# Attention's output projection: head sums made beside the scores, and a third pair of k with seven block products

## The chip, the cores and the metric

The kernel runs on one core of a Trainium2 chip. The time is the device time of one execution, in microseconds (us); three runs of the kernel before are given by their median. One further execution was profiled, and all rows quoted below come from it. Its engines: PE multiplies matrices, DVE and ACT work element by element, POOL and SP mostly issue transfers. Each engine takes its instructions in the order in which they stand in its own list, and waits at the first whose inputs are not there.

## The reference, cut to what matters

Two layers over 256 positions of width 2048. Layer 0 mixes tokens with a gated spatial MLP; layer 1, the one that matters here, with attention over 16 heads in blocks of 128 queries, whose outputs go through one square projection. After each mixer comes a layer norm, then a gated MLP with a short convolution, then another norm.

```python
def chunk_causal_attention(q_nope, q_rope, k_nope, k_rope, v):
    for qb in range(S // Q_BLOCK):
        ...
        s = s.astype(jnp.float32) * SM_SCALE
        ...
        p = jax.nn.softmax(s, axis=-1).astype(v.dtype)
        outs.append(jnp.einsum('bhqk,bkhd->bqhd', p, v[:, :k_end]))
...
    o = chunk_causal_attention(q_nope, q_rope, k_nope, k_rope, v)
    return o.reshape(B, S, MLA_HEADS * V_DIM) @ w_out
...
x = layer_norm(ALPHA * x + m, ln_mix_g[i], ln_mix_b[i])
f = conv_ffn(x, ffn_w_up[i], ffn_conv_w[i], ffn_conv_b[i], ffn_w_down[i])
```

Everything is float32, and the result must agree with that.

## The kernel before, in words

**Products.** A float32 product is made of rounded parts: each operand is split into a high part (a cast on ACT, L127) and a low part (a subtraction on DVE, L130), and three PE matmuls of 128x512 add hi*hi, lo*hi and hi*lo. Splitting the weights as they stream in is therefore the standing work of ACT and DVE. A chunk of weights is one 1 MB load into one of three "raw" buffers, and its parts (`wh`, `wl`) take two of 14 "big" slots, which also hold the attention's keys (`knT`), its outputs (`oT`), the residual and the normed input (`xhl`) of the next product.

**Eight or seven.** A chunk covers two blocks of k and 1024 columns, so 2x2 row blocks by 2x2 column blocks: eight block products, 24 matmuls. Marked `seven`, it is multiplied with seven block products (a Strassen-like form), 21 matmuls: then the weights' sums (`ts`, `th`, `tl`, L137 and L127/L130) must be made and split too, and so must sums of the other operand (`combine`: four DVE subtractions and additions by `turn`, a cast, a subtraction). `MO_SEVEN` names the pairs of k for which the second half of the attention's output projection does so.

**The stage around the change.** A loop over t runs the heads as a pipeline. Step t makes the scores of head t (`attend_a`: `sc` on PE; then ACT copies a piece, DVE masks, adds and takes maxima, ACT takes exponentials, DVE scales `p`), transposes p of head t-1 (`attend_b`: `pt` on PE, `pts` on ACT), multiplies head t-2 by the values (`attend_c`: `o` on PE, split into `oT`), and between these multiplies head t-4 by its weights for the first 1024 columns of the projection (`mo`, L232). The weights' chunks are numbered 298 to 305 for this half and 306 to 313 for the second 1024 columns (`mo_q`, `mo_p`, `mo_e`). With the last heads through, `sum_heads` makes the sums of the pairs 1 and 2 (heads 2, 3 and 4, 5), in the last two steps of the loop. Chunks 307 and 308 use them.

**The boundary behind it.** `boundary` finishes the four accumulators of the second half one after another (block 0 then block 1 of rows), adds each to the residual (`piece`: DVE L666 and a `BN_STATS`), aggregates (`start`: `BN_AGGR`, a root on ACT, a reciprocal), normalizes (`scale`: DVE L681), transposes (`put`: `lnt` on PE), applies gain and bias (`lny`, ACT L726) and splits (`xhl`, L729 and L730). Then `upf`, the first group of the next product, can start. Chunks 314 and up are its weights.

**What sets the order.** The instructions of an engine are not written out by hand: a scheduler orders them at build time by its own estimate of when inputs are ready, with earlier program text first. On the chip that order is fixed.

Of the kernel before, what the change touches and what calls it, by code (L numbers as in the profile page):

```python
# [8 lines left out]
F32 = mybir.dt.float32  # L9
# [6 lines left out]
P = 128  # L16
S = 256
# [7 lines left out]
H = 16  # L25
# [26 lines left out]
U_PAIRS = [[0, 1, 5, 7, 2, 6, 3, 4]] + [[0, 1, 2, 5, 3, 7, 4, 6]] * 5  # L52
U_SEVEN = [(2, 3)] + [(2, 3, 4)] * 4 + [(2, 3)]

MO_SEVEN = (1, 2)

T1, T2 = 6, 5
SLOTS = {"big": 14, "raw": 3, "side": 6}
# [153 lines left out]
def trunk(ctx: ExitStack, tc: tile.TileContext, x, xT, gm_in, gm_wout, ffn_up, ffn_dn,  # L212
# [5 lines left out]
    tp = ctx.enter_context(tc.tile_pool(name="tp", bufs=3))  # L218
# [6 lines left out]
    def slot(shape, name, dt=F32, tag="big"):  # L225
        return big.tile(shape, dt, tag=tag, name=name, bufs=SLOTS[tag])
# [47 lines left out]
    chunks += [(ml_b[i], 2048, "") for i in range(ml_b.shape[0])]  # L274
    chunks += [(ml_out[i], 2048, "seven" if i - 8 in MO_SEVEN else "") for i in range(ml_out.shape[0])]
    chunks += [(ffn_up[1, i], 2048, "") for i in range(n_up)]
# [13 lines left out]
    def turn(t, k1, k2):  # L290

        at = lambda k, b: k[:, b] if len(k.shape) == 3 else k[:, b * P : (b + 1) * P]
        tc.keep_in_program_order(nc.vector.tensor_tensor(t[:, 0], at(k1, 0), at(k1, 1), ALU.subtract))
        nc.vector.tensor_tensor(t[:, 1], at(k1, 1), at(k2, 1), ALU.subtract)
        nc.vector.tensor_tensor(t[:, 2], t[:, 1], at(k1, 0), ALU.subtract)
        nc.vector.tensor_tensor(t[:, 3], at(k2, 0), t[:, 2], ALU.add)

    def combine(name, o, k1, k2):


        t = tp.tile([P, 4, P], F32, tag="t2", name=f"xs{name}", bufs=T2)
        turn(t, k1, k2)
        o = o.rearrange("p (h s c) -> p h s c", h=2, s=4)
        nc.scalar.copy(o[:, 0], t)
        nc.vector.tensor_tensor(o[:, 1], t, o[:, 0].bitcast(F32), ALU.subtract)
        return [(o[:, 0, i], o[:, 1, i]) for i in (1, 2, 0, 3)]

    for j in range(4):
        t = slot([P, 4, S], f"xraw{j}", tag="side")
# [47 lines left out]
    def x_parts(xs, k, b):  # L357
        t = xs[k // 4]
        return (t[:, k % 4, b * P : (b + 1) * P], t[:, k % 4, S + b * P : S + (b + 1) * P])

    def prod_b(acc, parts, hi, lo, pieces, first, last):

        xh, xl = parts
        for f, (o, w) in enumerate(pieces):
            mm(acc[f][:, :w], xh, hi[:, o : o + w], first, False)
            mm(acc[f][:, :w], xl, hi[:, o : o + w], False, False)
            mm(acc[f][:, :w], xh, lo[:, o : o + w], False, last)
# [385 lines left out]
    for gi in range(6):  # L753
# [3 lines left out]
        for c, p in enumerate(V_PAIRS[gi]):  # L757
            a = [[x_parts(xhl, 2 * p + j, b) for j in range(2)] for b in range(2)]
            got = feed.next()
            if p in V_SEVEN[gi]:  # L760
                acc.seven(a, xc[p], *got)
                if p == V_SEVEN[gi][-1]:
                    rest = acc.rest()
            elif gi == 0 and c < 2:
                acc.first(a, *got, c == 0)
            else:
                acc.eight(a, *got)
            if gi == 0 and p in V_SEVEN[1]:
                x4 = xraw[p // 2]
                room = xc_room[len(xc) // 2][:, len(xc) % 2, :]  # L770
                xc[p] = combine(p, room, x4[:, 2 * (p % 2)], x4[:, 2 * (p % 2) + 1])
            if c == 2 and gi > 0:
                stats(gi - 1)
            if c == 4 and gi == 0:
                nc.sync.dma_start(cst, consts)
                nc.sync.dma_start(rope_sb, ropes)
                nc.sync.dma_start(lnrow, ln_rows.rearrange("r (k p) -> (r k) p", p=P))
                nc.sync.dma_start(brow[0:NG, :], b_s.rearrange("o (g i) -> (o g) i", g=NG))
            if c == 7 and gi == 5:
                wTg = []  # L780
                for i in range(4):
                    t = tp.tile([P, 2, P], F32, tag="t1", name=f"wT{i}", bufs=T1)
                    nc.gpsimd.dma_start(t, w_sT[:, 2 * i : 2 * i + 2, :])
                    nc.gpsimd.memset(t[64:P, :, 0:64], 0.0)
                    wTg += [t[:, 0, :], t[:, 1, :]]
        vt = slot([P, 2, 1024], f"v{gi}", tag="side")
        for i, (n, t) in enumerate(zip(DIRECT, rest)):
            o = vt[:, i // 2, (i % 2) * 512 : (i % 2) * 512 + 512]
# [80 lines left out]
    for g in range(6):  # L869
# [26 lines left out]
        for i, t in enumerate(rest):  # L896
            o = v[g][:, i // 2, i % 2 * 512 : i % 2 * 512 + 512]
# [146 lines left out]
    for b in range(2):  # L1044
# [3 lines left out]
        t = tp.tile([P, 4, ROPE], F32, tag="t1", name=f"kr2_{b}", bufs=T1)  # L1048
# [117 lines left out]
    def attend_b(h):  # L1166

        p = probs[h]
        pt = bank(f"pt{h}")
        for j in range(3):  # L1170
            nc.tensor.transpose(pt[:, j * P : (j + 1) * P], p[:, j * P : (j + 1) * P], ident)  # L1171
        pts = tp.tile([P, 3 * P], F32, tag="t2", name=f"pts{h}", bufs=T2)
        nc.scalar.copy(pts, pt[:, : 3 * P])
        probs[h] = pts

    def attend_c(h):
        if h % 4 == 0:
            oT.append(slot([P, 4, 512], f"oT{h // 4}", F32R))
        pts = probs.pop(h)
        o = bank(f"o{h}")  # L1180
        c = slice(h * P, (h + 1) * P)
        mm(o[:, 0:S], vv[0][:, c], pts[:, 0:S], True, False)
        mm(o[:, P:S], vv[1][:, c], pts[:, S : 3 * P], False, True)
        hi = oT[h // 4][:, h % 4, 0:S]
        nc.scalar.copy(hi, o[:, 0:S])
        nc.vector.tensor_tensor(oT[h // 4][:, h % 4, S : 2 * S], o[:, 0:S], hi.bitcast(F32), ALU.subtract)

    for hf in range(2):
# [13 lines left out]
        for b in range(2):  # L1202
            for f in range(2):
                c = slice(hf * 1024 + f * 512, hf * 1024 + (f + 1) * 512)
# [7 lines left out]
    mo_sums, mo_room = {}, []  # L1212

    def sum_heads(c):

        if len(mo_sums) % 2 == 0:
            mo_room.append(slot([P, 2, 8 * P], f"mos{c}", F32R))
        x = oT[c // 2][:, 2 * (c % 2) : 2 * (c % 2) + 2]
        raw = tp.tile([P, 2, S], F32, tag="t2", name=f"mor{c}", bufs=T2)
        nc.vector.tensor_tensor(raw, x[:, :, 0:S].bitcast(F32), x[:, :, S : 2 * S].bitcast(F32), ALU.add)  # L1220
        mo_sums[c] = combine(f"mo{c}", mo_room[-1][:, len(mo_sums) % 2, :], raw[:, 0], raw[:, 1])

    for t in range(3, H + LAG):
        k = t - LAG
        if k >= 0:
            if k % 2 == 0:
                hi, lo = feed.next()
            w = slice((k % 2) * 1024, (k % 2) * 1024 + 1024)
        if 3 < t < H:
            attend_a(t)  # L1230
        if k >= 0:
            prod_b(acc[0], x_parts(oT, k, 0), hi[:, w], lo[:, w], halfp, k == 0, k == KD - 1)
        if t < H + 2:
            attend_c(t - 2)
        if k >= 0:
            prod_b(acc[1][:1], x_parts(oT, k, 1), hi[:, w], lo[:, w], halfp[:1], k == 0, k == KD - 1)
        if t - 1 < H:
            attend_b(t - 1)
        if 0 <= t - H - 1 < len(MO_SEVEN):
            sum_heads(MO_SEVEN[t - H - 1])  # L1240
        if k >= 0:
            prod_b(acc[1][1:], x_parts(oT, k, 1), hi[:, w], lo[:, w], halfp[1:], k == 0, k == KD - 1)
    ln.begin()
# [4 lines left out]
    mo = Banks("mo1", DIRECT + OWN)  # L1248
    acc = [[mo.acc[DIRECT[2 * b + f]] for f in range(2)] for b in range(2)]
    late = []  # L1250
    for c in range(8):
# [7 lines left out]
        a = [[x_parts(oT, 2 * c + j, b) for j in range(2)] for b in range(2)]  # L1259
        if c in MO_SEVEN:  # L1260
            mo.seven(a, mo_sums[c], *got)
        else:
            mo.eight(a, *got)
        if c == MO_SEVEN[-1]:
            for j, t in enumerate(mo.rest()):
# [107 lines left out]
```

## Time and profile before

| what | us |
|---|---|
| median of 3 runs | 2464.81 (2464.58 to 2466.5) |
| the profiled execution, its own time | 2465.45 |
| its span in the trace | 2463.7 |
| PE busy | 2456.6 |
| DVE busy | 2070.3 |
| ACT busy | 1464.1 |

In rows of a timeline the first number is the start, the second how long the row took (where a row ends in x2 or more, from the first start to the last end), then engine, line, operation and operands; a bracket at the end says how long the engine was idle before and what ended that. All starts count from the start of the span. Matmuls overlap: one takes 0.39 us, and the next starts some 0.23 us after it. The stage of the change lies between about 1637 and 1760 us. The granted PE clock was 1.00 throughout.

### The profile page before, as it was taken

What the parts mean: (1) busy time and instruction counts of PE and PEld (TensorE: products, weight loads), DVE (VectorE), ACT (ScalarE), POOL (GpSimd) and SP (SyncE); (2) the same over time, 40 slices, a digit from 0 to 9 for tenths busy, and PEclk for the clock granted to TensorE, in tenths of its full rate; (3) what the DMA queues carried; (4) which work ended last, traced back from release to release, by engine and by line L of the source; (5) the groups of instructions that cost most, each with busy time, mean ns of one, the idle gap of its engine ahead of it and who ended that gap; (6) DMA issues with size and microseconds to landing.
All of it is one profiled execution on the core that took longest, in us unless ns stands there. A gap on an engine that the chain in (4) does not pass through costs nothing. (4 is left out here: it accounts for less than half of the span.)

```text
span 2463.7 us, 32505 instructions
## 1 busy us (share of the span) xinstructions
PE 2456.6 (100%) x12488; PEld 2091.5 (85%) x12488; DVE 2070.3 (84%) x2762; ACT 1464.1 (59%) x1972; POOL 104.2 (4%) x202
## 2 busy tenths in 40 slices
PE   9999999999999999999999999999999999999999
PEld 7888888888888888888888888988888888888887
DVE  7999999989897788787777997868798787878798
ACT  6666665566565666556655566665665665555453
POOL 0000000000000000000000000000000000000000
PEclk9999999999999999999999999999999999999999
DMA  7555666656665778777868885543588787867885
GB/s 291 202 208 205 227 202 204 205 188 205 222 208 202 235 283 330 287 283 293 324 216 319 301 303 186 184 163 123 211 281 303 267 310 298 300 265 271 303 323 204
DMA packets 116428, 611.94 MB, mean 248 GB/s; under 512 B 10648, under 2 KB 10912, under 8 KB 75184
## 3 DMA queue, kind: packets, MB, share of 16 engines
q1 hardware_dynamic: 90128, 462.47, 52.9%
q0 software_dynamic: 26144, 147.39, 15.9%
q8 instruction: 98, 1.61, 0.3%
q14 instruction: 58, 0.48, 0.1%
HBM read 544.75 MB, written 65.06 MB: 248 GB/s over the span
## 5 line engine op out<-in xcount | busy, mean ns | idle before, releaser
L130 DVE TENSOR_TENSOR wl<-raw,wh 128x1024 fp32r<-128x1024 f32 (+4 forms) x643 | 956.4, 1502 | 164.2 <-ACT wh L127 120.6
L127 ACT CAST wh<-raw 128x1024 fp32r<-128x1024 f32 (+4 forms) x643 | 808.0, 1279 | 357.1 <-PE up L232 86.9
L232 PE MATMUL up<-xhl,wh 128*128 128x512 f32 x2624 | 611.4, 390 | 0.0
L232 PEld LDWEIGHTS up<-xhl,wh 128*128 128x128 f32 x2624 | 487.7, 188 | 97.5
L232 PEld LDWEIGHTS up<-xhl,wl 128*128 128x128 f32 x2624 | 325.8, 192 | 6.4
L232 PE MATMUL up<-xhl,wl 128*128 128x256 f32 x2624 | 328.1, 283 | 0.0
L127 ACT CAST th<-ts 128x1536 fp32r<-128x1536 f32 (+1 forms) x142 | 146.6, 1051 | 112.0 <-DVE ts L137 83.0
L232 PE MATMUL ub<-wh,xhl 128*128 128x512 f32 x576 | 179.7, 393 | 0.3 <-DVE u0w L454 0.3
L130 DVE TENSOR_TENSOR tl<-ts,th 128x1536 fp32r<-128x1536 f32 (+1 forms) x142 | 167.7, 1218 | 10.4 <-ACT th L127 3.4
L232 PEld LDWEIGHTS ub<-wh,xhl 128*128 128x128 f32 x576 | 108.1, 188 | 24.9 <-issue 1.9
L232 PE MATMUL ub<-wl,xhl 128*128 128x512 f32 x288 | 112.2, 390 | 0.0
L137 DVE TENSOR_TENSOR ts<-ts,raw 128x512 f32<-128x512 f32 x142 | 97.4, 686 | 1.5
L137 DVE TENSOR_TENSOR ts<-raw 128x1024 f32<-128x1024 f32 x71 | 86.5, 1219 | 7.3 <-PE ub L232 3.8
L232 PE MATMUL v_q<-wh,xhl 128*128 128x512 f32 x224 | 70.6, 391 | 0.4 <-ACT wh L127 0.4
L232 PEld LDWEIGHTS ub<-wl,xhl 128*128 128x128 f32 x288 | 54.1, 188 | 11.3
L232 PE MATMUL v_p<-wh,xhl 128*128 128x512 f32 x192 | 59.9, 389 | 0.0
L232 PEld LDWEIGHTS v_q<-wh,xhl 128*128 128x128 f32 x224 | 42.0, 188 | 10.1 <-ACT wh L127 1.5
L390 DVE TENSOR_TENSOR h_1a<-up,lo_1a 128x256 f32<-128x256 f32 x41 | 17.2, 419 | 33.0 <-ACT lo_1a L388 32.8
L390 DVE TENSOR_TENSOR h_0a<-up,lo_0a 128x256 f32<-128x256 f32 x41 | 17.2, 419 | 32.5 <-ACT lo_0a L388 32.5
L154 DVE TENSOR_TENSOR praw<-praw 128x512 f32<-128x512 f32 x64 | 43.9, 686 | 0.6
L726 ACT ACTIVATE lny<-lnt,lncol 128x128 f32<-128x128 f32 x96 | 36.3, 467 | 13.1 <-PE lnt L722 13.0
L232 PE MATMUL v_q<-wl,xhl 128*128 128x512 f32 x112 | 43.8, 391 | 0.1
(1885 smaller groups left out, 4418.6 us busy)
## 6 DMA issues: line engine op xcount, KB each, us to landing
raw<-in_ffn_up_dram SPq DMA_DIRECT2D x172, 1024.0 KB, 7.1
raw<-in_gm_in_dram SPq DMA_DIRECT2D x93, 1024.0 KB, 5.3
raw<-in_ffn_dn_dram SPq DMA_DIRECT2D x68, 1024.0 KB, 7.0
raw<-in_gm_wout_dram SPq DMA_DIRECT2D x48, 1024.0 KB, 5.2
praw<-in_ffn_dn_dram POOLq DMA_DIRECT2D x16, 1024.0 KB, 13.9
keptth<-pth POOLq DMA_DIRECT2D x16, 1024.0 KB, 8.1
kepttl<-ptl POOLq DMA_DIRECT2D x16, 1024.0 KB, 8.9
fth<-keptth POOLq DMA_DIRECT2D x16, 1024.0 KB, 9.6
```

Of the source, the lines that this page charges most:

```text
L127: cast = self.nc.scalar.copy(hi, raw)
L130: self.nc.vector.tensor_tensor(lo, raw, hi.bitcast(F32), ALU.subtract)
L137: add = lambda o, a, b: self.nc.vector.tensor_tensor(o, a, b, ALU.add)
L154: add = lambda o, a, b: pin(nc.vector.tensor_tensor(o, a, b, ALU.add))
L232: recent[0] = nc.tensor.matmul(o, l, r, start=start, stop=stop, skip_group_check=True)
L390: nc.vector.tensor_tensor(h, acc[:, 0:S], lo, ALU.add)
L726: nc.scalar.activation(y[:, j], t[:, j * P : (j + 1) * P], AF.Identity, bias=lncol[:, o : o + 1], scale=lncol[:, g : g + 1])
```

## The change

Three pairs instead of two get seven block products: chunk 309 (pair 3, heads 6 and 7) joins 307 and 308. The sums are no longer made in the last steps of the loop but in its middle, at t = 8, 10 and 12, for the pairs 1, 2 and 3. Their scratch (`raw`, `t`) no longer comes from the small rotating buffers "t2" but from a "big" slot of its own, `mot`, beside the slot `mos` of the results. So two big slots are taken for pairs 1 and 2, and two more for pair 3, and they are taken while the scores are still under way.

```diff
-MO_SEVEN = (1, 2)
+MO_SEVEN = (1, 2, 3)
...
-    def combine(name, o, k1, k2):
-        t = tp.tile([P, 4, P], F32, tag="t2", name=f"xs{name}", bufs=T2)
+    def combine(name, o, k1, k2, t=None):
+        if t is None:
+            t = tp.tile([P, 4, P], F32, tag="t2", name=f"xs{name}", bufs=T2)
         turn(t, k1, k2)
...
         if len(mo_sums) % 2 == 0:
             mo_room.append(slot([P, 2, 8 * P], f"mos{c}", F32R))
+            mo_room.append(slot([P, 4, 512], f"mot{c}"))
         x = oT[c // 2][:, 2 * (c % 2) : 2 * (c % 2) + 2]
-        raw = tp.tile([P, 2, S], F32, tag="t2", name=f"mor{c}", bufs=T2)
+        n = len(mo_sums) % 2
+        raw = mo_room[-1][:, 2 * n].rearrange("p (j c) -> p j c", j=2)
+        t = mo_room[-1][:, 2 * n + 1].rearrange("p (s c) -> p s c", s=4)
         nc.vector.tensor_tensor(raw, x[:, :, 0:S].bitcast(F32), x[:, :, S : 2 * S].bitcast(F32), ALU.add)
-        mo_sums[c] = combine(f"mo{c}", mo_room[-1][:, len(mo_sums) % 2, :], raw[:, 0], raw[:, 1])
+        mo_sums[c] = combine(f"mo{c}", mo_room[-2][:, n, :], raw[:, 0], raw[:, 1], t)
...
-        if 0 <= t - H - 1 < len(MO_SEVEN):
-            sum_heads(MO_SEVEN[t - H - 1])
+        if t % 2 == 0 and (t - 6) // 2 in MO_SEVEN:
+            sum_heads((t - 6) // 2)
```

The diff is short, but the scheduler answers it with another order from head 9 to the end of the boundary. In the built program the slots `mos1` and `mot1` are those that chunk 300 leaves at the end of step 9, `mos3` is the one that the last keys (`knT3`) leave after the scores of head 15, and chunk 303 is given the slot of the keys `knT2`, which are read until the scores of head 11. Three places matter for the prediction.

**First place: DVE, heads 10 and 11.** `sc`, `p` and `mx` carry the number of the head; `wl303` is the low part of chunk 303. Before:

```order
L1163 TENSOR_SCALAR p9_13993<-p9_13993,mx9_13992 128x256
L130 TENSOR_TENSOR wl303_14038<-raw303_13842,wh303_14037 128x1024 [waits DMAHW6_49,PE_49,Activation_49]
L130 TENSOR_TENSOR wl303_14038<-raw303_13842,wh303_14037 128x1024 [waits Activation_49]
L1152 TENSOR_SCALAR sc10_14045<-sc10_14045,negc_187 128x2x64 [waits Activation_49]
L1153 TENSOR_TENSOR p10_14047<-sc10_14045,sl10_14056 128x128 [waits DVE_49]
```

With the change:

```order
L1164 TENSOR_SCALAR p10_14056<-p10_14056,mx10_14055 128x256
L306 TENSOR_TENSOR mos1_13988<-mot1_13989,mos1_13988 128x512 [waits Activation_49]
L130 TENSOR_TENSOR wl303_14047<-raw303_13842,wh303_14046 128x1024 [waits DMAHW6_49,DVE_49,Activation_49]
L130 TENSOR_TENSOR wl303_14047<-raw303_13842,wh303_14046 128x1024 [waits Activation_49]
L1153 TENSOR_SCALAR sc11_14108<-sc11_14108,negc_187 128x2x64 [waits Activation_49]
```

The split of chunk 303 has moved from ahead of head 10's softmax to between the softmaxes of heads 10 and 11, with the sums of pairs 1 and 2 ahead of it.

**Second place: ACT, heads 14 and 15.** `oT3` is the output of heads 12 to 15. Before:

```order
L1159 ACTIVATE p14_14248,mx14_14247<-p14_14248,mx14_14247 128x128 [waits DVE_49]
L1159 ACTIVATE p14_14248,mx14_14247<-sc14_14246,mx14_14247 128x256
L1185 CAST oT3_14275<-o12_14276 128x256 [waits PE_49]
L1150 COPY sl15_14304<-sc15_14293 128x128 [waits PE_49]
L127 CAST wh306_14339<-raw306_14144 128x1024 [waits DMAHW1_49]
```

With the change:

```order
L1160 ACTIVATE p14_14273,mx14_14272<-p14_14273,mx14_14272 128x128 [waits DVE_49]
L305 CAST mos3_14205<-mot3_14206 128x512 [waits PE_49]
L127 CAST wh305_14263<-raw305_14052 128x1024 [waits DMAHW0_49,PE_49]
L127 CAST wh305_14263<-raw305_14052 128x1024
L1160 ACTIVATE p14_14273,mx14_14272<-sc14_14271,mx14_14272 128x256
L1186 CAST oT3_14300<-o12_14301 128x256 [waits DVE_49]
```

Between the two exponentials of head 14 now stand the cast of the third sum, which waits for PE (its slot is that of the keys read by the scores of head 15), and the two casts of chunk 305.

**Third place: DVE at the boundary.** `mo1_e` and `mo1_q4` are the accumulators of row block 1; `lnmv2_0` and `lnrs2_0` are mean and scale of block 0; L681 (now L682) normalizes, and its first result is what PE transposes. Before:

```order
L674 BN_AGGR lnmv2_0_14712<-lnst2_0_14446 128x2 [waits DVE_49]
L666 TENSOR_TENSOR res1_1_11812<-res1_1_11812,mo1_e_14458 128x512 [waits PE_49]
L353 RECIPROCAL lnrs2_0_14716<-lnrs2_0q_14714 128x1 [waits Activation_49]
L669 BN_STATS lnst2_1_14447<-res1_1_11812 128x6 [waits DVE_49]
L681 TENSOR_SCALAR res1_0_10982<-res1_0_10982,lnmv2_0_14712,lnrs2_0_14716 128x512 [waits DVE_49]
L681 TENSOR_SCALAR res1_0_10982<-res1_0_10982,lnmv2_0_14712,lnrs2_0_14716 128x512
L130 TENSOR_TENSOR wl316_14665<-raw316_14654,wh316_14664 128x1024 [waits DMAHW3_49,PE_49,Activation_49]
L130 TENSOR_TENSOR wl316_14665<-raw316_14654,wh316_14664 128x1024 [waits Activation_49]
L681 TENSOR_SCALAR res1_1_11812<-res1_1_11812,lnmv2_0_14712,lnrs2_0_14716 128x512
L666 TENSOR_TENSOR res1_1_11812<-res1_1_11812,mo1_q4_14459 128x512 [waits PE_49]
L730 TENSOR_TENSOR xhl3_0_14738<-lny2_0_0_14747,xhl3_0_14738 128x4x128 [waits Activation_49]
```

With the change:

```order
L130 TENSOR_TENSOR wl316_14676<-raw316_14665,wh316_14675 128x1024 [waits DMAHW3_49,PE_49,Activation_49]
L130 TENSOR_TENSOR wl316_14676<-raw316_14665,wh316_14675 128x1024 [waits Activation_49]
L670 BN_STATS lnst2_0_14452<-res1_1_11812 128x6 [waits DVE_49]
L667 TENSOR_TENSOR res1_1_11812<-res1_1_11812,mo1_e_14464 128x512
L675 BN_AGGR lnmv2_0_14723<-lnst2_0_14452 128x2 [waits DVE_49]
L667 TENSOR_TENSOR res1_1_11812<-res1_1_11812,mo1_q4_14465 128x512 [waits PE_49]
L670 BN_STATS lnst2_1_14453<-res1_1_11812 128x6 [waits DVE_49] x2
L354 RECIPROCAL lnrs2_0_14727<-lnrs2_0q_14725 128x1 [waits Activation_49]
L675 BN_AGGR lnmv2_1_14839<-lnst2_1_14453 128x2 [waits DVE_49]
L682 TENSOR_SCALAR res1_0_10982<-res1_0_10982,lnmv2_0_14723,lnrs2_0_14727 128x512 [waits DVE_49]
```

The split of chunk 316 and the last piece of block 1 (`mo1_q4`, the accumulator that PE finishes last of all) have moved ahead of the first normalization of block 0. Behind these rows stand the other seven normalizations, and only then `xhl3_0`. On PE the four transposes of block 0's first quarter, which stood inside the last run of `mo1_q4` matmuls, stand behind the whole of it.

## Prediction

> **What bounds the kernel now.** I read the page's busy times first, then what PE waited for, then the stage of the change in slices of 10 us.
>
> ```profile
> PE 2456.6 (100%) x12488; PEld 2091.5 (85%) x12488; DVE 2070.3 (84%) x2762; ACT 1464.1 (59%) x1972; POOL 104.2 (4%) x202
> PE upf L232 <- ACT xhl L729: 0.2, 1, 0.2
> core 0: us, PE busy (x) PEld busy (x) DVE busy (x) ACT busy (x) POOL busy (x), PEclk, DMA share, GB/s
> 1660.00:1670.00 10.00, 10.00 (x60) 8.69 (x59) 7.30 (x23) 5.56 (x16) 0.00 (x0) 1.00 0.30 105
> 1710.00:1720.00 10.00, 10.00 (x46) 8.28 (x45) 9.96 (x12) 6.21 (x6) 0.00 (x0) 1.00 0.23 75
> 1720.00:1730.00 10.00, 10.00 (x46) 8.28 (x45) 10.00 (x14) 5.56 (x7) 0.00 (x0) 1.00 0.84 320
> 1740.00:1750.00 10.00, 9.81 (x48) 7.75 (x46) 8.39 (x14) 5.76 (x11) 0.00 (x0) 1.00 0.51 193
> ```
>
> PE is the bound: 2456.6 of 2463.7 us, and its one wait behind 1740 us within this stage is 0.2 us. So a time that PE loses here is not given back later, and a matmul left out is time won, as long as PE still finds its inputs. The slices show how thin that is. Beside the scores DVE is busy 7.3 of 10 us; in the second half of the projection, 9.96 and 10.00. There DVE has no room, and PE goes on only because DVE's work is ready just in time. I therefore follow PE and DVE side by side to the point where they meet, the boundary.
>
> **What is left out.** Chunk 309 goes from 24 matmuls to 21. Six take 1.36 us in the chain of waits:
>
> ```profile
> 1728.26 1.36 PE mo_p L232 x6
> ```
>
> So one is 0.227 us, and three are 0.7 us. That is all there is to win, 0.03% of the time, and only if PE sets the end of the stage.
>
> **What is added to DVE.** In the second half a seven-block chunk and wide chunks stand back to back in the timeline:
>
> ```profile
> 1712.52 1.21 DVE L137 TENSOR_TENSOR ts<-raw 128x1024 f32<-128x1024 f32 x1
> 1714.37 1.75 DVE L130 TENSOR_TENSOR wl<-raw,wh 128x1536 fp32r<-128x1536 f32 x1
> 1718.91 6.89 DVE L130 TENSOR_TENSOR wl<-raw,wh 128x1024 fp32r<-128x1024 f32 x6
> 1725.73 0.68 DVE L453 TENSOR_TENSOR mo1u<-mo_p,mo1p 128x512 f32<-128x512 f32 x1
> ```
>
> Chunk 308 takes 1718.91 - 1712.52 = 6.39 us, three wide ones 1725.73 - 1718.91 = 6.82, or 2.27 each. Chunk 309 as a seven thus costs DVE 4.1 us more, in slices that are already full. The sums go the other way:
>
> ```profile
> 1696.69 0.68 DVE L1220 TENSOR_TENSOR mor<-oT 128x512 f32<-128x512 f32 x1
> 1697.40 0.29 DVE L293 TENSOR_TENSOR xsmo<-mor 128x128 f32<-128x128 f32 x1
> 1700.69 0.68 DVE L305 TENSOR_TENSOR mos<-xsmo,mos 128x512 fp32r<-128x512 f32 x1
> ```
>
> A pair is two rows of 0.68 and four of 0.29, some 2.2 us with their overlap. Two pairs, 4.4 us, leave 1697 to 1707; three, 6.6 us, enter steps 10 to 15.
>
> **Beside the scores.** DVE has 2.7 us idle in 10 there, but it is idle inside the softmax, which is a chain. For head 11, in order of time over the three engines, and at the end the head with the least room:
>
> ```profile
> 1670.91 0.40 PE L232 MATMUL sc<-krT,qrT 128*128 128x256 f32 x2
> 1672.04 0.27 ACT L1150 COPY sl<-sc 128x128 f32<-128x128 f32 x1
> 1672.92 0.35 DVE L1152 TENSOR_SCALAR sc<-sc,negc 128x128 f32<-128x128 f32 x1
> 1676.03 0.55 DVE L1163 TENSOR_SCALAR p<-p,mx 128x128 f32<-128x128 f32 x2
> 1678.59 0.49 PE L1171 MATMUL pt<-ident,p 128*128 128x128 f32 x3
> ...
> 1682.07 0.54 DVE L1163 TENSOR_SCALAR p<-p,mx 128x128 f32<-128x128 f32 x2
> 1683.29 0.49 PE L1171 MATMUL pt<-ident,p 128*128 128x128 f32 x3
> ```
>
> Head 11 has 2.0 us of room (1676.6 to 1678.6), the tightest 0.7. With the change chunk 303 sits in the slot of the keys that head 11 reads until 1671.3, so its casts come behind that, head 10's exponentials and the cast of the sum, at about 1672.5; its first cast ends at 1673.5, its split on DVE (2.27) at 1675.8, and head 11's mask, now behind it, starts at 1675.9 instead of 1672.92. That is 3.0 later against 2.0 of room: PE waits about 0.7 us, since some of the later idle time in the chain closes up. The same happens with chunk 304 ahead of head 13 (about 0.4) and on ACT at head 14, where the sum's cast waits for head 15's scores with chunk 305, head 14's second exponential and the cast of `oT3` queued behind it, for which PE's transposes and next products wait (about 0.4). I take 1.5 us in all. Bounds: 0, if all of it fits the room; 6.6 - 4 x 0.7 = 3.8, if four heads have only the least room.
>
> **The boundary.** Now PE and DVE, each from rows of the end of the stage:
>
> ```profile
> 1746.53 0.66 PE L722 MATMUL lnt<-ident,res 128*128 128x128 f32 x4
> 1748.88 0.39 PE L232 MATMUL mo_q<-wl,oT 128*128 128x512 f32 x1
> 1749.90 0.50 PE L232 MATMUL upf<-wh,xhl 128*128 128x512 f32 x1 [0.19 <-ACT xhl L729]
> 1750.95 0.50 PE L232 MATMUL upf<-wh,xhl 128*128 128x512 f32 x1
> ...
> 1704.82 1.28 DVE L668 SCALAR_TENSOR_TENSOR res<-res,mo 128x512 f32<-128x512 f32 x2
> 1742.81 0.26 DVE L674 BATCH_NORM_AGGREGATE lnmv<-lnst 128x2 f32<-128x24 f32 x1
> 1744.62 0.69 DVE L666 TENSOR_TENSOR res<-res,mo_e 128x512 f32<-128x512 f32 x1 [1.54 <-PE mo_e L232]
> 1745.95 0.99 DVE L681 TENSOR_SCALAR res<-res,lnmv,lnrs 128x512 f32<-128x512 f32 x2
> 1746.88 2.36 DVE L130 TENSOR_TENSOR wl<-raw,wh 128x1024 fp32r<-128x1024 f32 x2
> ```
>
> Before, DVE aggregates block 0 at 1742.81, even waits 1.54 us for PE, normalizes at 1745.95, and PE transposes at 1746.53 with matmuls still to do (until 1749.1). Gain, bias and split run under these, and PE flows into `upf`.
>
> *DVE.* From the first `res` (1704.82) to the end of the aggregate (1743.07) it takes 38.25 us. With the change, between the same rows: chunk 309, 4.1 more; chunk 316's split, now ahead of the aggregate, 2.3; chunk 307's low part, now behind the first `res`, 1.7; `res<-mo_e`, now ahead, 0.6; less a cast's remainder `mos`, 0.6, and the one small gap, 0.3. That is 46.0. It starts 1.5 later, at 1706.3, so the aggregate ends at 1752.3.
>
> *PE.* Its last matmul ended its turn at 1749.1; now 1.5 later for the scores, 0.7 earlier for the three, 0.4 earlier because the transposes have left: 1749.5. So where DVE comes to `res<-mo1_q4`, PE has been through for about 2.5 us: the sums' saving on PE is lost, and DVE sets the end. From there, in DVE's order: that `res` and two BN_STATS (3 x 0.6), reciprocal and aggregate (0.4), the first normalization (0.5): 2.7 us, and the transposes start at 1755.1, with nothing left to do on PE.
>
> *Behind the transposes.* For the last quarter of block 0 the path is not overlapped:
>
> ```profile
> 1753.58 0.60 PE L722 MATMUL lnt<-ident,res 128*128 128x128 f32 x4
> 1754.22 1.50 ACT L726 ACTIVATE lny<-lnt,lncol 128x128 f32<-128x128 f32 x4 [0.35 <-PE lnt L722]
> 1755.75 0.63 ACT L729 CAST xhl<-lny 128x512 fp32r<-128x512 f32 x1
> 1756.41 0.69 DVE L730 TENSOR_TENSOR xhl<-lny,xhl 128x512 fp32r<-128x512 f32 x1 [0.31 <-ACT xhl L729]
> ```
>
> From `lnt` to the end of `xhl` are 1757.1 - 1753.58 = 3.5 us. ACT's order now has one more `lny` (0.4) ahead of the cast, and DVE has seven normalizations (half of 0.99 each, 3.5) ahead of `xhl`, which end about when the cast does. I take 4.0. The second `upf` matmul, the first that needs the low part, then starts at 1759.1 instead of 1750.95. **The sum is +8.2 us**: 1.5 from the scores, the rest from the boundary. On the profiled execution's 2465.45 it gives 2473.6, on the median, 0.6 lower, 2473.0, which is my forecast.
>
> Bounds: if DVE came to `res<-mo1_q4` no later than PE's last matmul and the scores cost nothing, PE would be through at 1748.0, the transposes start 0.2 + 2.7 later at 1750.9, and `upf` at 1754.9: +4.0, from the order of the boundary alone. Above: scores 3.8 instead of 1.5, +10.5; and DVE's two new waits (chunk 307's `tl` for a slot of chunk 306, chunk 316 for its load), which no row prices. The nearest is the one wait of a weights' cast for PE's `mo_q` in this stage:
>
> ```profile
> ACT wh L127 <- PE mo_q L232: 2.4, 1, 2.4
> ```
>
> 2.4 more would make it +12.9. I give these waits nothing, since both inputs come due within half a microsecond of their turn.
>
> **A rule and a row.** PE would do no matmuls but a few transposes from 1749.5 to 1758, which no stretch of this trace shows. The nearest row is the program's beginning:
>
> ```profile
> 1.31 4.45 PE L232 MATMUL warm<-idle 128*128 128x512 bf16 x10 [1.31 <-POOL idle L283]
> 2.00:4.00 2.00, 2.00 (x6) 0.76 (x5) 0.00 (x0) 0.02 (x1) 0.49 (x1) 1.00 0.81 282
> ```
>
> Ten matmuls from idle take 4.45 us, 0.45 each with the last one's end, though the slice of 2 us says a granted clock of 1.00 and later ones follow each other at 0.227. A PE that starts again after a pause at that pace for as long would lose 4.45 x (1 - 0.227 / 0.45) = 2.2 us. The Trainium skill, page "TensorE: Matmul & The Clock Gate", section "Why this matters for your kernels", says just this: pauses of more than about 3 us between bursts put the clock back to half. By that rule the sum would be +10.4; by the rows alone, which have no such pause, +8.2. No run here shows it yet.
>
> **The rivals.**
> - *The clock falls in the pause.* +10.4 on the median: 2475.2. For it: the pause is longer than any in the trace, and the beginning is slow. Against: the profile grants 1.00 even at the beginning, so its clock column may not show it. Chance 0.2.
> - *DVE catches up* before the boundary: the waits that it has in the second half swallow the seven, only the order costs. Decides: whether `res<-mo1_q4` waits for PE. Price +4.0 to +4.9: 2469.3. Against it, slices with no idle time. 0.1.
> - *Not slower: the reordered boundary is covered.* If DVE were a full 4 us ahead of PE, as it was 1.5 ahead before (the wait for `mo_e`), and the first normalization cost nothing behind `mo1_q4`, the boundary would take what it took, and PE would keep its 0.7 and lose only in the scores: 2464.8 + 0.8 = 2465.6, or 2464.1 with none lost there. It decides where DVE's last row ahead of the normalization does not wait for PE's last matmul. Against it: DVE runs its rows in the order shown, as the timeline before does row by row. 0.05.
> - *The scores cost more*, 3.8 instead of 1.5: 2475.3. For it: three engines wait in a ring at head 14. 0.1.
>
> My forecast has 0.55 (its own range 2471.2 to 2474.6). A measurement of this kernel tells 0.2%, or 4.9 us, from no change. Faster by more than that would need seven times the saving: 0.03. Within: the covered boundary and most of DVE catching up: 0.13. Slower: 0.84. The range from 2468.8 to 2476.9 holds the catching up and the clock, and leaves out the covered boundary and the sum of all upper bounds.
>
> **What would show it.** Of the changed kernel: PE idle between the last `mo_q` and the second `upf` of 9 us with few transposes, put down to `res` and `xhl`; DVE full from 1706 to about 1755, with `res<-mo_q` of block 1 ahead of the first normalization and no wait for PE there; PE waits at `pt` around heads 11, 13 and 14 of 1.5 us together; the first `upf` matmuls at 0.23 us, or twice that if the clock falls. I am wrong if `res<-mo_q` waits for PE (then +4 to +5), or if the stretch from `lnt` to `upf` has matmuls in it.

## The result

The changed kernel takes 2474.77 us (median of 5 runs, 2474.56 to 2475.33), the kernel before in the same set 2464.66. That is 10.1 us more, a ratio of 1.004 with a 95% interval of 1.0029 to 1.0051. The forecast was 2473.0, slower; its range from 2468.8 to 2476.9 holds the time. The forecast's own narrower range ended at 2474.6, and the rival "the clock falls in the pause" stood at 2475.2: the time lies between the two, 0.2 us above the first and 0.4 below the second, so it is nearer to the rival than to the forecast. The runs below say why.

### The profile page after: what moved, and what is told of

Its sections match the earlier page's. It is cut to its first block, busy times and chain, and to the rows that moved or that the text cites. A ratio compares the mean times of both kernels' runs of the same rounds, so it can differ in the third digit from the quotient of the medians.

```text
span 2473.6 us, 32511 instructions
## 1 busy us (share of the span) xinstructions
PE 2459.4 (99%) x12485; PEld 2091.6 (85%) x12485; DVE 2075.1 (84%) x2772; ACT 1466.0 (59%) x1974; POOL 104.1 (4%) x202
## 5 line engine op out<-in xcount | busy, mean ns | idle before, releaser
L232 PEld LDWEIGHTS v_q<-wh,xhl 128*128 128x128 f32 x224 | 42.0, 188 | 10.1 <-ACT wh L127 1.5
L232 PE MATMUL upf<-wh,xhl 128*128 128x512 f32 x128 | 43.7, 415 | 1.7 <-ACT xhl L730 1.7
L232 PE MATMUL mo<-wh,oT 128*128 128x512 f32 x128 | 43.2, 413 | 0.2 <-ACT oT L1186 0.2
```

The costliest lines, as they stand in the source:

```text
L232: recent[0] = nc.tensor.matmul(o, l, r, start=start, stop=stop, skip_group_check=True)
```

## The profile after

The profiled execution took 2475.33 us, its span is 2473.6. The page's busy times, and then what PE waited for between 1600 and 1800 us (in all, how often, the longest):

```profile
PE 2459.4 (99%) x12485; PEld 2091.6 (85%) x12485; DVE 2075.1 (84%) x2772; ACT 1466.0 (59%) x1974; POOL 104.1 (4%) x202
```

```profile
PE lnt L723 <- DVE res L682: 4.4, 1, 4.4
PE upf L232 <- ACT xhl L730: 1.7, 1, 1.7
PE mo_q L232 <- ACT th L127: 0.9, 1, 0.9
PE mo L232 <- ACT oT L1186: 0.2, 1, 0.2
```

Three matmuls are gone, and PE, which had waited 0.2 us in this stage, now waits 7.2 there. PE's busy time has even grown by 2.8 us: its matmuls became longer somewhere. The slices of 10 us show where (PE, PEld, DVE, ACT, POOL busy, the granted clock, DMA):

```profile
1750.00:1760.00 10.00, 4.41 (x16) 3.65 (x17) 7.92 (x19) 4.76 (x13) 0.00 (x0) 0.61 0.33 107
1760.00:1770.00 10.00, 10.00 (x45) 8.13 (x44) 4.44 (x5) 6.22 (x13) 0.00 (x0) 0.88 0.00 0
```

PE stands idle for more than half of 1750 to 1760 while DVE is full to about 1757, and the granted clock falls to 0.61 and 0.88 on the mean. Now the timeline of the changed kernel, first PE:

```profile
1664.41 0.34 PE L232 MATMUL sc<-knT,qnT 128*128 128x256 f32 x2
...
1706.34 0.39 PE L232 MATMUL mo_q<-wh,oT 128*128 128x512 f32 x1
...
1749.16 0.39 PE L232 MATMUL mo_q<-wl,oT 128*128 128x512 f32 x1
1753.93 1.97 PE L723 MATMUL lnt<-ident,res 128*128 128x128 f32 x8 [4.38 <-DVE res L682]
1757.56 0.80 PE L232 MATMUL upf<-wh,xhl 128*128 128x512 f32 x1 [1.66 <-ACT xhl L730]
1758.15 1.06 PE L723 MATMUL lnt<-ident,res 128*128 128x128 f32 x4
1758.86 0.78 PE L232 MATMUL upf<-wh,xhl 128*128 128x512 f32 x1
...
1769.06 0.38 PE L723 MATMUL lnt<-ident,res 128*128 128x128 f32 x2
```

and the rows of the kernel before that belong to the first, second and last of these:

```profile
1665.51 0.34 PE L232 MATMUL sc<-knT,qnT 128*128 128x256 f32 x2
...
1706.31 0.39 PE L232 MATMUL mo_q<-wh,oT 128*128 128x512 f32 x1
...
1759.51 0.27 PE L722 MATMUL lnt<-ident,res 128*128 128x128 f32 x1
```

The scores of head 10 come ahead of anything that the change moves, and stand 1.10 us earlier in this trace than in that of before (two executions differ by so much). So 1.10 is added to a time of after when it is compared with before; for the other runs the same anchor gives 0.22 to 1.24. And DVE, from the first `res` of the second half to the boundary:

```profile
1704.49 1.37 DVE L669 SCALAR_TENSOR_TENSOR res<-res,mo 128x512 f32<-128x512 f32 x2 [1.68 <-PE mo L232]
...
1711.82 2.36 DVE L130 TENSOR_TENSOR tl<-ts,th 128x1536 fp32r<-128x1536 f32 x2 [0.71 <-PE mo_q L232]
...
1747.73 2.36 DVE L130 TENSOR_TENSOR wl<-raw,wh 128x1024 fp32r<-128x1024 f32 x2 [0.52 <-ACT wh L127]
...
1751.20 0.26 DVE L675 BATCH_NORM_AGGREGATE lnmv<-lnst 128x2 f32<-128x24 f32 x1
1751.37 0.63 DVE L667 TENSOR_TENSOR res<-res,mo_q 128x512 f32<-128x512 f32 x1
...
1753.40 1.84 DVE L682 TENSOR_SCALAR res<-res,lnmv,lnrs 128x512 f32<-128x512 f32 x4
...
1757.54 0.69 DVE L731 TENSOR_TENSOR xhl<-lny,xhl 128x512 fp32r<-128x512 f32 x1 [0.27 <-ACT xhl L730]
```

`res<-mo_q` of block 1 has no bracket: it did not wait for PE, which had been through for 1.8 us (1749.16 + 0.39). DVE sets the end, as forecast. In one clock:

| place | before | after, with 1.10 added | later by | forecast |
|---|---|---|---|---|
| first `mo_q` of the second half | 1706.31 | 1707.44 | 1.1 | 1.5 |
| end of DVE's aggregate of block 0 | 1743.07 | 1752.56 | 9.5 | 9.2 |
| first transposes of block 0 | 1746.53 | 1755.03 | 8.5 | 8.6 |
| second `upf` | 1750.95 | 1759.96 | 9.0 | 8.2 |
| first transpose of block 1 | 1759.51 | 1770.16 | 10.7 | 8.2 |

Up to the transposes the forecast holds within 0.4 us. Behind them 2.5 us more are lost than it had: 0.8 by the second `upf`, the rest in the matmuls that follow it.

## The experiments

*Theory*: the third seven's 4.1 us on DVE make the scheduler turn the boundary round, and DVE's lateness is what PE waits for. *Rivals*: the sums and slots beside the scores cost; the order doesn't matter, only DVE's total work does; the slow matmuls behind the pause are late inputs and no clock. Each run was timed beside the kernel before on the same chip; "over before" is against that.

**The sums alone, and the third pair alone.** The first is the change with `MO_SEVEN` back at two pairs, the second is the kernel before with three, its sums in the last steps of the loop and in the small buffers:

```diff
-MO_SEVEN = (1, 2, 3)
+MO_SEVEN = (1, 2)
```

```diff
-MO_SEVEN = (1, 2)
+MO_SEVEN = (1, 2, 3)
```

> The sums of pairs 1 and 2 are made beside the scores, in slots of their own, as in the change; there is no third pair (chunk 309 has eight block products). Theory (the third pair's work on DVE turns the boundary round, the scores cost little): the normalization of block 0 stands ahead of the last piece of block 1 again, PE is covered at the boundary, and only the scores cost, 0.4 to 1.1 us: 2465.1 to 2465.8. Rival (the sums and the two big slots beside the scores are what costs): most of the 10.1 us stays, 2472 or more.

> The kernel before with a third pair alone: three sums in the last steps of the loop, in the small buffers. Theory: nothing is lost beside the scores, but DVE starts the second half some 2 us later than before (the third sum), the boundary has the order of the change, and PE stands idle there: 9 to 12 us over before, 2473.5 to 2476.5, with a slow stretch of matmuls behind the pause. Rival (the sums and slots beside the scores cost): 0.7 us under before to 1 over, 2464.0 to 2465.7.

Measured: sums alone 2465.24, 0.7 over before (ratio 1.0003, 0.9994 to 1.0012); third pair alone 2474.54, 10.0 over (1.004, 1.0025 to 1.0055). PE's waits with the third pair alone:

```profile
PE lnt L722 <- DVE res L681: 4.4, 1, 4.4
PE upf L232 <- ACT xhl L729: 1.7, 1, 1.7
PE mo_q L232 <- ACT th L127: 1.3, 1, 1.3
```

They are nearly those of the change, and the order of DVE's rows at the boundary is that of the change too, though no sum is made beside the scores and no big slot for scratch is taken. With the sums alone that order is gone, and PE waits nowhere at the boundary. The third pair carries the loss. What the scores cost with the sums alone, 0.9 us at the first `mo_q`, agrees with its 0.7 over before, though 0.7 by itself is within the noise; in the total of the change, where DVE sets the end, it can't be seen.

**The third pair's sum without its seven.** Sums and slots as in the change, but chunk 309 has eight block products:

```diff
-        if c in MO_SEVEN:
+        if c in MO_SEVEN[:2]:
             mo.seven(a, mo_sums[c], *got)
```

(and the same for the chunk's mark `seven` and for the fold behind the last of them).

> The change with all three sums and their four slots, but chunk 309 multiplied with eight block products: PE has its three matmuls again, DVE 4.1 us less, and the sum of pair 3 isn't used. Theory (DVE's 4.1 us for the third seven decides): the boundary has the order of the kernel before and is covered, and 0.4 to 1.4 us over before remain for the scores: 2464.9 to 2466.0. Rival (the third sum, its slots and the queue on ACT at head 14 are what costs): 2470 or more.

Measured: 2465.05, 0.2 over before (1.0001, 0.9992 to 1.0011). In its timeline the transposes stand inside the run of `mo_q` again, 9 us earlier than with the change:

```profile
1744.35 0.39 PE L232 MATMUL mo_q<-wh,oT 128*128 128x512 f32 x1
1744.58 0.60 PE L723 MATMUL lnt<-ident,res 128*128 128x128 f32 x4
1744.93 0.48 PE L232 MATMUL mo_q<-wh,oT 128*128 128x512 f32 x1
```

So it is neither the sums nor their slots; it is the chunk multiplied with seven.

**The load alone, and the load taken away.** The kernel before with 4.7 us more on DVE and nothing else; and the change with 4.7 us less. The second leaves something out: the low parts of chunks 313 and 315 are not computed, and ACT copies the whole weights in their place.

```diff
-        self.nc.vector.tensor_tensor(lo, raw, hi.bitcast(F32), ALU.subtract)
+        for _ in range(2 if self.split in (309, 310) else 1):
+            self.nc.vector.tensor_tensor(lo, raw, hi.bitcast(F32), ALU.subtract)
```

```diff
-        self.nc.vector.tensor_tensor(lo, raw, hi.bitcast(F32), ALU.subtract)
+        if self.split in (313, 315):
+            self.nc.scalar.copy(lo, raw)
+        else:
+            self.nc.vector.tensor_tensor(lo, raw, hi.bitcast(F32), ALU.subtract)
```

> The kernel before, with the low parts of chunks 309 and 310 computed twice: 4.7 us more on DVE where the third seven has 4.1, and nothing else of the change. Theory: the built order has chunk 316's split ahead of the aggregate and the last piece ahead of the first normalization, as with the change; transposes at about 1752.4 and the second upf at about 1756.2 instead of 1750.95: 5 to 8 us over before, 2469.8 to 2473, the more if the clock falls. Rival (the load alone doesn't turn the boundary round): under 2466.

> The change, with DVE's subtraction for chunks 313 and 315 left out: ACT copies the whole weights in place of their low parts (so for these two chunks the low part is not computed). DVE has 4.7 us less before the boundary, and nobody has them instead but ACT, which is idle 4 of 10 us there. Theory (DVE's load of the third seven is what costs): the order of the kernel before, the aggregate 4 to 5 us earlier than with the change, PE with matmuls of mo_q behind the first transposes, 1.1 us at the scores and about 1 at the boundary left, clock 1.00: 2466.0 to 2468.0. Rival (the third seven costs by its five slots or by PE's order, not by DVE's time): 2471 or more.

Measured: load added 2472.63, 8.3 over before (1.0032, 1.0019 to 1.0044); load taken away 2466.32, 2.0 over (1.0007, 0.9997 to 1.0016). Load added, PE:

```profile
1752.07 1.97 PE L723 MATMUL lnt<-ident,res 128*128 128x128 f32 x8 [3.61 <-DVE res L682]
```

Load taken away, PE:

```profile
1747.44 0.66 PE L726 MATMUL lnt<-ident,res 128*128 128x128 f32 x4
1747.85 0.49 PE L235 MATMUL mo_q<-wh,oT 128*128 128x512 f32 x1
...
1750.59 0.50 PE L235 MATMUL upf<-wh,xhl 128*128 128x512 f32 x1 [0.19 <-ACT xhl L733]
1751.32 0.49 PE L235 MATMUL upf<-wh,xhl 128*128 128x512 f32 x1
```

With the load alone the kernel before gets the change's boundary: on DVE the split of chunk 316 stands ahead of the aggregate and the last piece of block 1 (at 1749.64) ahead of the first normalization (1751.49), and PE has its transposes at 1752.29 in the clock of before (1752.4 was expected), behind a pause of 3.6 us, and a slow stretch. With the load taken from the change the wait of 4.4 us is gone. What is left, 1.6 us at the second `upf`, is nearly the scores' 1.1 and the 0.9 for `th`, less 0.7. DVE's time is the cause, shown from both sides: added, it brings 8.3 us of loss; taken away, it leaves 2.0 of 10.1. It acts in two ways at once, and these two runs don't part them: DVE comes late, and the scheduler answers its time with another order.

**The order pinned.** The last piece of block 1 is held behind the first two normalizations (`scaled` keeps these); in the second of these runs chunk 316's split is made later too:

```diff
-                nc.vector.tensor_tensor(r, r, acc, ALU.add)
+                p = nc.vector.tensor_tensor(r, r, acc, ALU.add)
+                if (self.idx, b, f) == (2, 1, 3):
+                    order(p, self.scaled[1])
```

```diff
-        got = feed.next(splits=2 if left > 5 else 3, loads=2)
+        got = feed.next(splits=2 if left > 5 or left == 0 else 3, loads=2 if left else 3)
```

> The change, with one row of DVE moved by force: the last piece of row block 1 stands behind the first two normalizations of block 0; chunk 316's split stays ahead of them. Theory (the order at the boundary costs): the transposes start about 1.3 us earlier, xhl comes behind three normalizations instead of eight, and the pause of PE is about 3.1 us instead of 4.4: 2 to 3.5 us back, 2471.3 to 2472.8. Rival (DVE's total work sets the end, whatever its order): 2474.8, the same as the change.

> The change, with the last piece behind the normalizations as in the run before and chunk 316's split put behind them too. Theory: DVE aggregates 2.3 us earlier, about when PE ends its last matmul; PE waits about 1 us for the transposes and 3.5 to 4 us from there to the second upf, so 5 to 6 us come back, 2468.8 to 2469.8; if the pause of about 1 us doesn't lower the clock, the upf matmuls follow each other at 0.23 us from the first. Rival (the clock falls whenever PE has only transposes to do): slow matmuls here too, and 2470.5 to 2471.5. Rival (DVE's total work): 2474.8.

Measured: 2474.26, 9.7 over before (1.0039, 1.0024 to 1.0054), and 2469.64, 5.1 over (1.002, 1.001 to 1.0029). The first missed: 0.5 us came back, not 2 to 3.5. Its PE:

```profile
1749.37 0.39 PE L232 MATMUL mo_q<-wl,oT 128*128 128x512 f32 x1
1752.92 1.11 PE L726 MATMUL lnt<-ident,res 128*128 128x128 f32 x8 [3.16 <-DVE res L685]
1756.09 0.80 PE L232 MATMUL upf<-wh,xhl 128*128 128x512 f32 x1 [2.06 <-ACT xhl L733]
1757.39 0.78 PE L232 MATMUL upf<-wh,xhl 128*128 128x512 f32 x1
```

The transposes do start earlier, and the second `upf` by 1.8 us (1758.20 against 1759.96 in the clock of before). But the slow stretch has only moved: the transposes still run at full pace (1.11 for eight against 1.97), and the matmuls behind the second wait at half. With both pinned:

```profile
1750.49 1.11 PE L726 MATMUL lnt<-ident,res 128*128 128x128 f32 x8 [0.30 <-DVE res L685]
1753.67 0.50 PE L232 MATMUL upf<-wh,xhl 128*128 128x512 f32 x1 [2.06 <-ACT xhl L733]
1754.39 0.51 PE L232 MATMUL upf<-wh,xhl 128*128 128x512 f32 x1
```

No slow matmul is left in this execution, the aggregate stands 2.8 us earlier than with the last piece alone pinned (1749.39 against 1752.21 in the clock of before; chunk 316's split takes 2.36), and half of the loss has come back. The ten executions fall into two groups: five with a granted clock of 1.000 over the whole run take 2468.26 to 2469.21 us, five with 0.999 take 2470.07 to 2470.48. So in half of them the clock fell for a while after all; none of these was profiled. The 5.1 us over before lie between the two groups. They stay in this order; how much of them is DVE's lateness, and whether a third order would save more, was not tried.

**The pause filled.** The change, with matmuls of zeros where PE would stand idle; the order on DVE stays but for one normalization, which now stands behind the first `xhl` (there the change's DVE waited 0.27 us for ACT in any case; the call that makes the first transposes is written behind the last `mo_q`, where the built order has them anyway):

```diff
             t = bank(f"lnt{i}_{b}_{f}")
+            for _ in range({(2, 0, 0): 17, (2, 0, 1): 6}.get((i, b, f), 0)):
+                hot = mm(t, still[:, 0:P], still, True, True)
...
```

> The change, with matmuls of zeros in PE's pause whose result is overwritten: 17 (17 x 0.227 = 3.9 us) between the last mo_q and the first transposes, 6 between the two first groups of transposes; the order on DVE is that of the change. Theory (the slow matmuls behind the pause are the clock, which falls because PE does too little in some 3.4 us): granted clock 1.00 throughout, the eight transposes shorter, the upf matmuls at 0.23 us from the first, and 1.8 to 2.5 us come back: 2472.3 to 2473.0. Rival (they are slow because their inputs come late): the same slow matmuls and 2474.8.

Measured: 2472.19, 7.4 over before (1.003, 1.0019 to 1.0042), 2.6 under the change, a little more than the 1.8 to 2.5 expected. PE:

```profile
1749.76 3.62 PE L232 MATMUL lnt<-still 128*128 128x512 bf16 x16
1754.08 0.66 PE L732 MATMUL lnt<-ident,res 128*128 128x128 f32 x4 [0.70 <-DVE res L687]
...
1757.84 0.48 PE L232 MATMUL upf<-wh,xhl 128*128 128x512 f32 x1
```

From the first transpose to the second `upf` are 3.8 us instead of 4.9, and the granted clock is 1.00 in every slice. Inputs were not late; it was the clock, and it cost 2.6 us.

**Two low parts on POOL.** Meant to take the load off DVE without leaving anything out; first on the change, then on the kernel before with the third pair and the pinned last piece, which might have beaten both:

```diff
-        self.nc.vector.tensor_tensor(lo, raw, hi.bitcast(F32), ALU.subtract)
+        low = self.nc.gpsimd if self.split in (313, 315) else self.nc.vector
+        low.tensor_tensor(lo, raw, hi.bitcast(F32), ALU.subtract)
```

> The change, with the low parts of chunks 313 and 315 made by POOL instead of DVE, 4.7 us of DVE's work before the boundary; nothing else is moved by hand. Theory (DVE's load of the third seven, through the order that it brings about, is what costs): the first normalization stands ahead of the last piece again, with matmuls of mo_q behind the first transposes; left are 1.1 us at the scores, 0.9 for th, less 0.7: 2465.5 to 2467, and up to 2 more if POOL's parts come late. Rival (the load on DVE isn't the cause, but the new slots and the boundary's waits): 2470 or more.

> The kernel before with the third pair, the sums in the last steps of the loop, the low parts of chunks 313 and 315 on POOL, and the last piece of block 1 held behind the first two normalizations. Theory: no loss beside the scores, 1.3 us for th as in the run with the third pair alone, 0.7 less for the three matmuls, boundary covered: 2464.3 to 2466. If the saving of the three matmuls came through whole: 2464.0. Rival (POOL's two parts come late or slow DVE down): 2467 or more.

Measured: 2471.92, 7.1 over before (1.0029, 1.0018 to 1.004), and 2472.06, 7.2 over (1.0028, 1.0018 to 1.0039). Both missed, and the first lies where the rival was expected, at 2470 or more. POOL's and then DVE's timeline of the first:

```profile
1735.53 5.16 POOL L131 TENSOR_TENSOR wl<-raw,wh 128x1024 fp32r<-128x1024 f32 x2 [201.14 <-ACT wh L127]
1741.50 5.92 POOL L131 TENSOR_TENSOR wl<-raw,wh 128x1024 fp32r<-128x1024 f32 x2 [0.81 <-ACT wh L127]
```

```profile
1735.66 0.68 DVE L457 TENSOR_TENSOR mo1u<-mo_p,mo1u 128x512 f32<-128x512 f32 x1
1736.85 1.62 DVE L662 SCALAR_TENSOR_TENSOR res<-res,mo1w 128x512 f32<-128x512 f32 x1
1738.39 2.85 DVE L662 SCALAR_TENSOR_TENSOR res<-res,mo1d 128x512 f32<-128x512 f32 x1
1741.76 6.74 DVE L131 TENSOR_TENSOR wl<-raw,wh 128x1024 fp32r<-128x1024 f32 x2
```

The built order did come back, with `mo_q` matmuls behind the first transposes. But while POOL subtracts, DVE's rows take 1.62 and 2.85 where the change had 0.68, and 6.74 for two halves of a chunk instead of 2.36: about 7.5 us lost for 4.7 taken away. PE then waits 2.5 us for POOL's parts and 0.9 for `th`, and its clock falls for 3.4 us (shown at the end). DVE was not relieved, so these two runs don't decide between the theory and the rival; the load was taken away cleanly only with ACT. Even so the first of them, with the order back, has 3.0 us less over before than the change.

None of these versions beats the kernel before. The most that the third pair could bring is 0.7 us.

## Why the prediction was right, step by step

*What is left out*: three matmuls fewer, as said; 0.7 us that never showed, since DVE sets the end.

*What is added to DVE*: right, and the cause. From the first `res` to the end of the aggregate 46.0 us were forecast; after shows 1751.46 - 1704.49 = 47.0. The 1.0 more is DVE's two new waits, 0.71 and 0.52, which the working priced at nothing. Against them DVE started only 0.8 us later than before (1704.49 + 1.10 against 1704.82) and not 1.5. Two errors of opposite sign: that the end of the aggregate came out within 0.3 us is in part luck. The load alone does most of it, and the load taken away undoes most of it.

*Beside the scores*: the right stage, too large: 1.1 instead of 1.5. Nor does it show as PE's waits at `pt`, as forecast. PE itself waits 0.2 us there, for `oT`; its weight loads wait 1.3 us for `oT`, 0.5 for `p` and 0.3 for `pts` between 1664 and 1707. It also hardly mattered, which the working missed: it was carried into DVE's start, but with the third pair alone nothing is lost at the scores and the total is the same within 0.1 us. Nor was head 14's cast of the third sum it: with two sums alone 0.9 of the 1.1 is there.

*The boundary*: right in mechanism and within 0.4 us up to the transposes. Two sizes were off. PE's wait for `th` of chunk 309, 0.9 us, was missing. It moved PE's last matmul, but not the end. And the 4.0 us from transposes to the second `upf` held at full clock (3.8 with the pause filled); at the clock that PE really had they were 4.9.

*A rule and a row*: the fallen clock is the term that was missing from the sum. The likeliest case took a full clock, the rival took 2.2 us for a fallen one; filling the pause gives back 2.6. The Trainium skill's rule ("TensorE: Matmul & The Clock Gate", "Why this matters for your kernels") was nearer than the rows alone, and the trace agrees with it: a pause of 4.4 us, and a clock of 0.50 behind it. Another run, at the end of this text, lost its clock with no pause above 1.6 us, so the length in that rule is not a limit here. A chance of 0.2 for that rival was too low: the profile's own row of a slow start spoke for it, and the counter-argument (the clock column stays at 1.00 at the beginning) does not hold inside the run, where the column shows the fall.

*The rivals*: DVE did not catch up. The boundary was not covered, and its order alone was not to blame: with both rows pinned 5.1 us remain. That the scores cost more than forecast fell with their 1.1 us.

## What to carry to other kernels

Before you trade matmuls for element work, look at the slices in which the element engine already has no idle time, and follow its lateness to the next place where the matmul engine has nothing else to do; three matmuls (0.7 us) against 4.1 us of DVE is lost there. Ask also what a pause does behind itself: here it cost 2.6 us of half clock beyond its own length. Work that is moved away from a full engine can cost that engine more than it takes off: here 7.5 us for 4.7, with POOL beside DVE.

## What the runs showed of the hardware

*The clock falls by stretches.* In slices of 0.5 us, the edges of the slow stretch with the change,

```profile
1752.00:1752.50 0.50, 0.00 (x0) 0.00 (x0) 0.50 (x1) 0.00 (x0) 0.00 (x0) 0.71 0.94 393
...
1762.00:1762.50 0.50, 0.50 (x3) 0.40 (x2) 0.50 (x1) 0.00 (x0) 0.00 (x0) 0.55 0.00 0
```

and with the last piece pinned:

```profile
1754.50:1755.00 0.50, 0.00 (x0) 0.00 (x0) 0.50 (x2) 0.50 (x2) 0.00 (x0) 0.88 0.05 16
1761.50:1762.00 0.50, 0.50 (x3) 0.35 (x2) 0.50 (x2) 0.00 (x0) 0.00 (x0) 0.80 0.00 0
```

A mean of 0.71 between 1.00 and 0.50 puts the fall at 1752.2, one of 0.55 the rise at 1762.4: 10.2 us. In the other run it is 1754.9 to 1761.7, 6.8 us. These are three and two times 3.41, and a third run below has one of 3.4. The Trainium skill ("TensorE: Matmul & The Clock Gate", "What's actually happening") has a free-running window of that length, and the traces agree. What they add is that PE need not be idle all the while: in the run with the last piece pinned the 3.41 us ahead of the fall hold eight transposes, 1.11 us of work, and the clock fell all the same; the 3.41 us ahead of these (1748.05 to 1751.47) hold matmuls until 1749.76, 1.7 us, and did not bring it down, though the wait of 3.2 us began in them. Nor does this hang on transposes, which might not count as work. In the first run with POOL ordinary matmuls stand between two shorter pauses:

```profile
1737.97 0.50 PE L233 MATMUL mo_q<-wl,oT 128*128 128x512 f32 x1 [0.97 <-POOL wl L131]
...
1740.74 0.79 PE L233 MATMUL mo_q<-wl,oT 128*128 128x512 f32 x1 [1.57 <-POOL wl L131]
```

```profile
1740.00:1740.50 0.50, 0.00 (x0) 0.00 (x0) 0.50 (x1) 0.12 (x1) 0.50 (x1) 0.94 0.00 0
...
1743.50:1744.00 0.50, 0.50 (x3) 0.42 (x2) 0.50 (x1) 0.18 (x1) 0.50 (x1) 0.64 1.00 426
```

By the same working the clock falls at 1740.4 and rises at 1743.9, and the 3.41 us ahead of the fall hold 1.20 us of matmuls (1737.97 to 1739.17). So what a pause costs depends on where it lies in the window and on what else lies there; I had thought of its length alone. The two groups of the kernel with both rows pinned fit this: the same program, and the group with the lower clock takes 1.6 us more on the mean, where one window at half pace would cost 1.7 (an estimate, half of 3.41).

*POOL holds up DVE where DVE reads two operands from SBUF.* In the rows above `res<-res,mo1d` and `wl<-raw,wh` are stretched while POOL subtracts; `mo1u<-mo_p,mo1u`, which reads an accumulator of PE, takes its 0.68 in the same time. The Trainium skill ("SBUF — State Buffer", "SBUF: two separate sides") says that the two engines share a port pair which one instruction locks for its whole length, a DVE instruction with two SBUF inputs among them. The trace agrees that such rows are held up, with 7.5 us lost on DVE beside 11.1 us of POOL; that the lock lasts for a whole instruction it does not show.
